# A depthwise convolution that reads its projection from PSUM instead of from a padded copy, in a two-layer hybrid backbone

## The chip, the cores and the metric

The kernel runs on one core of a Trainium2 chip. The metric is the device time of one execution in microseconds (us); the kernel before takes 1846.74 us, the median of 3 runs (1846.3 to 1852.83). Engines are called by the names of the profile: PE (matmuls and transposes), DVE, ACT, POOL, and SP, which issues most DMAs.

## The reference

Two layers over 512 tokens and 256 context tokens of 1024 columns. Each layer normalises and modulates its input and projects it for three groups of heads: neighbourhood attention, a bidirectional state-space scan (SSD), and grouped-query attention (GQA). Then come an output projection and a gated feed-forward block. The change lies in the SSD group, where 1024 projected channels pass a five-tap convolution along the tokens and a silu:

```python
def depthwise_conv(x, w, bias):
    y = lax.conv_general_dilated(x, w[:, None, :], window_strides=(1,),
                                 padding=[(SSD_CONV // 2, SSD_CONV // 2)],
                                 dimension_numbers=('NWC', 'WIO', 'NWC'),
                                 feature_group_count=x.shape[-1])
    return y + bias
...
    def prep(v):
        z, xbc, dt_raw = jnp.split(v, [SSD_WIDTH, SSD_WIDTH + SSD_CONV_CH], axis=-1)
        xbc = jax.nn.silu(depthwise_conv(xbc, conv_w, conv_b))
        xs, bm, cm = jnp.split(xbc, [SSD_WIDTH, SSD_WIDTH + SSD_GROUPS * SSD_STATE], axis=-1)
...
    z, xs, bm, cm, dt = prep(u)
    zc, xsc, bmc, cmc, dtc = prep(u_c)
```

`prep` runs on the tokens and on the context apart, so each of the two sequences has its own zero padding of two columns at either end.

## The kernel before, in words

Channels lie on the 128 partitions and tokens along the free dimension: 512 tokens, then 256 context tokens. The 1024 channels are eight blocks of 128, and `p_xbc(b)` (L749) makes block b in each layer; the text calls the blocks p0 to p7. In the second layer p6 and p7 need only the 512 tokens.

A block runs like this. `wblk` loads 1024 columns of weights and splits them into a high part `wh` (ACT, L326) and a low part `wl` (DVE, L327). `wh` and `wl` have three buffers each, so the split for a block must wait until PE has finished the block three before. `proj_ws` (L338) sums 48 matmuls, 24 of 512 columns and 24 of 256, into a tile `S` of PSUM (24 matmuls where the context is left out). `S` has two buffers. ACT copies the result into a padded tile `MA` in SBUF (L758 and L761), between zeros that DVE writes (L756, L757, L760). DVE makes the first tap with the bias (L763) and adds four more (L768), 770 columns each, into `MB`. ACT takes the tanh (L772) into `MA`, and DVE multiplies (1 + tanh) by the sum (L774 and L776, "the gates"), which with weights halved beforehand is silu. For p0 to p5 six transposes on PE (L785) and two copies on ACT (L791) bring the result into token order.

Other work is woven between the blocks. Three head transposes, tr0 to tr2, turn 128 columns of normalised GQA heads per token block with six or four PE transposes into an `S` tile too (L695); the result is read by ACT (L282) and DVE (L283), and only then is that `S` buffer free. Their inputs come from a rope and a norm on POOL and DVE (L683 to L688). `p_z` projects the gate z after and between the last blocks (L352), through small tiles `sm` and `PT`, with an evacuation on ACT (L805) and DVE (L806). In the first layer POOL and ACT also make the modulation of the second layer under all this: `mod_dots` multiplies 128x512 tiles on POOL (L228) and sums them on ACT (L229). Rows of POOL's L269 are a power that norms need.

Nobody writes the order by hand: a scheduler places every instruction on its engine by its own estimate of times, and each engine then runs its list strictly in that order. An instruction that must wait holds up all that is behind it on its engine.

Of the kernel before, what the change touches and what calls it, by code (L numbers as in the profile page):

```python
# [28 lines left out]
def hybrid_kernel(ctx: ExitStack, tc: tile.TileContext, a, out, dbg=None):  # L29
# [55 lines left out]
    class Split:  # L85
        """columns 0 .. 511 in one bank of PSUM, the others in another"""
# [11 lines left out]

    WB = {"wr": 2, "wh": 3, "wl": 3}
# [7 lines left out]
    # ---------------------------------------------------------- constants  # L107
# [42 lines left out]
    # ---------------------------------------------------------- modulation  # L150
# [8 lines left out]
    def mod_loads(l, c, tags):  # L159
        """512 columns of the modulation weights in tiles of the given tags, one or two k per tile"""  # L160
# [12 lines left out]
    def mod_chunk(l, c, w):  # L173
        """columns 512 c .. 512 c + 511 of the modulation; four row groups of the array take four k"""
# [21 lines left out]
    def mod_rows():  # L196
        """silu of both conditioning vectors as rows on every partition, in four tiles (vector, half)"""
# [11 lines left out]
    def mod_dots(l, c, rows, ptile, aside):  # L209
        """the same columns as mod_chunk by products along rows of the transposed weights"""  # L210
# [50 lines left out]
    # ---------------------------------------------------------- helpers  # L261
# [29 lines left out]
    def spread(rstd, n):  # L291
        """per-token values as a row on every partition"""
        pb = ps_sm()
        for tb in range(n // P):
            PE.matmul(
                pb[:, tb * P : (tb + 1) * P], lhsT=rstd[:, tb : tb + 1].to_broadcast([P, P]),
                rhs=ident, start=True, stop=True,
            )
        pbs = T(sb, "pr", 3, [P, NX])[:, 0:n]
        S.activation(pbs, pb[:, 0:n], AF.Copy)  # L300
        return pbs

    def make_h(l, xT, h, pbs, part, shi, sc):
        """norm, scale and shift of one part of the tokens"""
# [25 lines left out]
    def proj_ws(pt, wh, wl, xh, xl, nk, segs, ks=None):  # L330
        """pt[:, seg] = W^T x, W stationary (nk blocks of 128 rows)"""
# [13 lines left out]
    def proj_as(pt, ws, n, kper, xh, xl, t):  # L345
        """pt[:, :n] = x[t]^T W, activations stationary"""
# [28 lines left out]
    def attn(V2, xk, kts, qcols, bias, yout):  # L375
        """two heads and two blocks of queries; xk: range of x keys (or None); kts: key tiles for P V.
        Returns the steps of the four units: scores and softmax, transposes, and P V where one is complete"""
# [70 lines left out]
    # ---------------------------------------------------------- initial load and transpose  # L448
# [44 lines left out]
    for l in range(L):  # L493
# [9 lines left out]
        # ------------------------------------------------------ norm 1  # L503
# [6 lines left out]
        # ------------------------------------------------------ NA projections  # L510
# [77 lines left out]
        # ------------------------------------------------------ NA attention  # L588
# [50 lines left out]
        # ------------------------------------------------------ GQA projections  # L639
# [9 lines left out]
        def head_in(pt, i, t):  # L649
            """keep 128 columns (two heads) of token block t and their sums of squares"""  # L650
# [69 lines left out]
        # ------------------------------------------------------ GQA attention  # L720
# [24 lines left out]
        # ------------------------------------------------------ SSD: projections, conv  # L745
# [3 lines left out]
        def p_xbc(b):  # L749
            conly = last and b >= 6  # L750
            w = wblk(6 + b)
            pt = ps_s()
            proj_ws(pt, w[0], w[1], hh, hl, KB, xsegs if conly else asegs)
            cp = ma()
            wid = 512 if conly else 770
            V.memset(cp[:, 0:2], 0.0)  # L756
            V.memset(cp[:, 514:516], 0.0)  # L757
            S.activation(cp[:, 2:514], pt[:, 0:512], AF.Copy)  # L758
            if not conly:
                V.memset(cp[:, 772:774], 0.0)  # L760
                S.activation(cp[:, 516:772], pt[:, 512:768], AF.Copy)  # L761
            ac = mb()
            V.tensor_scalar(  # L763
                out=ac[:, 0:wid], in0=cp[:, 0:wid], scalar1=convw[l][:, b, 0:1], scalar2=convb[l][:, b : b + 1],
                op0=ALU.mult, op1=ALU.add,
            )
            for j in range(1, 5):
# [603 lines left out]
```

## Time and profile before

| | us |
|---|---|
| median of 3 runs | 1846.74 |
| lowest, highest | 1846.3, 1852.83 |
| span of the profiled execution | 1843.3 |
| first layer, from the last matmul of p1 to the last of z (164.0 to 301.4) | 137.4 |
| second layer, the same stretch (1211.43 to 1290.8) | 79.37 |

The span runs from the first to the last instruction of one execution; it is 3.4 us under the median of the runs. Over the whole span PE is busy 94%, DVE 60%, ACT 37% and POOL 23%. The two stretches in the table are those in which the eight blocks, the head transposes and z are made. [...]

### The profile page before, as it was taken

To read this page: it belongs to the slowest core of one execution; us is meant where nothing else is said; L and a number is where in the kernel's file an instruction comes from. 1 tells how busy PE (TensorE), PEld (TensorE's weight loads), DVE (VectorE), ACT (ScalarE), POOL (GpSimd) and SP (SyncE) were. 2 spreads that over 40 slices of the span, in tenths; PEclk is the share of its full clock that TensorE was granted. 3 is DMA by queue.
4 is the path that set the end of the run, shared out by engine and by line. 5 is a ranking of instruction groups with operands and counts; after the bars stand their busy time and mean duration, and the time that the engine had idled before them with its cause. 6 is when DMAs were issued, how large, how long until landed. Compare 5 with 4: busy or idle time off the path is not lost.

```text
span 1843.3 us, 26677 instructions
## 1 busy us (share of the span) xinstructions
PE 1737.0 (94%) x10146; PEld 1478.4 (80%) x10146; DVE 1104.0 (60%) x2209; ACT 681.5 (37%) x1386; POOL 423.1 (23%) x429
## 2 busy tenths in 40 slices
PE   7987778989999999999999999999899999999998
PEld 3887667777878888888888887989677788888887
DVE  4559996877475555455654576587786743333334
ACT  5554555556344221121112224334555442232222
POOL 0488886654010000000000002241653100000000
PEclk9998889989989999999999999999999999999999
DMA  9542526433123334333443454342631323333332
GB/s 368 201 139 103 163 89 186 140 90 106 56 75 115 114 115 126 103 116 107 124 129 102 130 163 139 96 131 79 183 105 53 108 90 93 99 96 92 103 100 83
DMA packets 94319, 221.66 MB, mean 120 GB/s; under 512 B 18416, under 2 KB 26224, under 8 KB 94192
## 3 DMA queue, kind: packets, MB, share of 16 engines
q1 hardware_dynamic: 78096, 204.65, 35.6%
q10 hardware_dynamic: 16096, 15.31, 2.5%
q8 instruction: 80, 1.31, 0.3%
q14 instruction: 47, 0.39, 0.1%
HBM read 198.49 MB, written 21.43 MB: 119 GB/s over the span
## 4 chain that ended last, share of the span: by engine, by line
PE 76%; DVE 11%; DMA 5%; ACT 3%; issue 2%; POOL 2%; SPq 0%; ACTq 0%; DVEq 0%; POOLq 0%
PE S L338 61%; PE sm L436 3%; DVE MB L768 2%; DMA wl<-crow 2%; PE PT L424 2%; DVE wl L327 1%; PE PT L338 1%; PE PT L352 1%; PE sm L352 1%; DMA wr<-in_mod_wT_dram 1%; DVE wh L892 1%; PE S L390 1%; ACT wh L326 1%; PE sm L913 1%; PE sm L914 1%
## 5 line engine op out<-in xcount | busy, mean ns | idle before, releaser
L326 ACT ACTIVATE wh<-wr 128x1024 fp32r<-128x1024 f32 (+3 forms) x214 | 207.6, 972 | 732.2 <-PE S L338 542.4
L327 DVE TENSOR_TENSOR wl<-wr,wh 128x1024 fp32r<-128x1024 f32 (+3 forms) x214 | 250.0, 1169 | 174.0 <-ACT wh L326 171.6
L269 POOL TENSOR_TENSOR tiny<-tiny,mhalf 128x2 f32<-128x2 f32 (+2 forms) x17 | 28.7, 1688 | 1067.5 <-DVE tiny L1160 1020.3
L338 PE MATMUL S<-HY,wh 128*128 128x512 f32 (+1 forms) x716 | 214.0, 357 | 5.9 <-ACT HY L318 4.1
L338 PE MATMUL S<-HY,wl 128*128 128x512 f32 (+1 forms) x716 | 214.5, 357 | 0.0
L338 PE MATMUL S<-HZ,wh 128*128 128x512 f32 (+1 forms) x716 | 212.8, 355 | 0.8 <-DVE HZ L319 0.8
L338 PE MATMUL S<-HS,wl 128*128 128x512 f32 (+1 forms) x716 | 213.1, 355 | 0.0
L338 PE MATMUL S<-HS,wh 128*128 128x512 f32 (+1 forms) x716 | 211.1, 353 | 0.0
L231 DVE CUSTOM_DVE_ANT_0 PT<-wr,XFB 128x512 f32<-128x512 f32 x112 | 75.5, 715 | 179.8 <-DMA wr<-in_mod_wT_dram 179.8
L338 PEld LDWEIGHTS S<-HY,wh 128*128 128x128 f32 x716 | 119.8, 192 | 27.2 <-ACT HY L318 4.4
L338 PEld LDWEIGHTS S<-HZ,wh 128*128 128x128 f32 x716 | 118.2, 191 | 21.7 <-DVE HZ L319 2.2
L338 PEld LDWEIGHTS S<-HS,wh 128*128 128x128 f32 x716 | 118.8, 191 | 20.2
L338 PEld LDWEIGHTS S<-HY,wl 128*128 128x128 f32 x716 | 118.8, 191 | 18.8
L338 PEld LDWEIGHTS S<-HS,wl 128*128 128x128 f32 x716 | 118.0, 190 | 18.6
L338 PE MATMUL S<-PHA,wh 128*128 128x512 f32 (+1 forms) x358 | 106.4, 355 | 0.0
L338 PE MATMUL S<-PHB,wh 128*128 128x512 f32 (+1 forms) x358 | 105.0, 351 | 0.0
L338 PE MATMUL S<-GX,wh 128*128 128x512 f32 (+1 forms) x400 | 97.2, 349 | 0.4 <-DVE KA L1114 0.4
L415 POOL TENSOR_SCALAR pr<-pr,tiny 128x640 f32<-128x640 f32 (+2 forms) x80 | 69.3, 869 | 84.0 <-DVE tiny L414 64.3
L768 DVE SCALAR_TENSOR_TENSOR MB<-MA,c,MB 128x770 f32<-128x770 f32 (+1 forms) x64 | 85.3, 1333 | 1.4
L228 POOL TENSOR_TENSOR KA<-QN,XFB 128x512 f32<-128x512 f32 x48 | 73.9, 1546 | 44.3 <-ACT XFB L205 23.5
L424 PE MATMUL PT<-c,pr 128*128 128x128 f32 x384 | 66.5, 289 | 13.4 <-POOL pr L415 4.6
L1261 DVE TENSOR_TENSOR MB<-S,MA 128x768 f32<-128x768 f32 (+1 forms) x42 | 34.6, 823 | 72.6 <-PE S L338 72.5
(402 smaller groups left out, 3911.7 us busy)
## 6 DMA issues: line engine op xcount, KB each, us to landing
wr<-in_mod_wT_dram SPq DMA_DIRECT2D x56, 512.0 KB, 3.7
wr<-in_w_gate_dram SPq DMA_DIRECT2D x44, 512.0 KB, 3.5
wr<-in_w_up_dram SPq DMA_DIRECT2D x44, 512.0 KB, 3.5
wr<-in_w_blk_dram SPq DMA_DIRECT2D x28, 512.0 KB, 3.6
wr<-in_w_down_dram SPq DMA_DIRECT2D x32, 448.0 KB, 3.3
QN<-in_mod_wT_dram SPq DMA_DIRECT2D x48, 256.0 KB, 3.3
wr<-in_w_out_dram SPq DMA_DIRECT2D x32, 256.0 KB, 2.6
wr<-in_w_down_dram SPq DMA_DIRECT2D x16, 512.0 KB, 3.4
```

What stands on the lines that cost most here:

```text
L228: G.tensor_tensor(out=p_, in0=wv, in1=x, op=ALU.mult)
L231: V.tensor_tensor_reduce(out=p_, in0=wv, in1=x, scale=1.0, scalar=0.0, op0=ALU.mult, op1=ALU.add, accum_out=acc[:, o : o + 1],)
L269: POW.tensor_tensor(out=y, in0=v, in1=mhalf[:, 0:n], op=ALU.pow)
L326: S.activation(hi, raw, AF.Copy)
L327: V.tensor_tensor(lo, raw, hi.bitcast(F32), ALU.subtract)
L338: ins = PE.matmul(pt[:, c0:c1], lhsT=w, rhs=xx[:, c0:c1], start=(k == (0 if len(order) == 1 else order[0]) and i == 0), stop=(k == (nk - 1 ...
L352: PE.matmul(pt[:, 0:n], lhsT=s, rhs=w[:, o : o + n], start=(k == 0 and i == 0), stop=(k == KB - 1 and i == 2),)
L415: G.tensor_scalar(out=p_, in0=p_, scalar1=m[:, 4:5], scalar2=1.0, op0=ALU.mult, op1=ALU.mult)
L424: PE.transpose(pt[:, k * P : (k + 1) * P], pr[j, qi][:, kk * P : (kk + 1) * P], ident)
L436: PE.matmul(pv[64 * j : 64 * j + 64, 0:P], lhsT=V2(kts[k], j), rhs=ph[j, qi][:, k, :], start=(k == 0), stop=(k == nkt - 1), tile_position= ...
L768: V.scalar_tensor_tensor(ac[:, 0:wid], cp[:, j : j + wid], convw[l][:, b, j : j + 1], ac[:, 0:wid], ALU.mult, ALU.add)
L1261: V.tensor_tensor(gg[:, c0:c1], pu[:, c0:c1], sg[:, c0:c1], ALU.mult)
```

## The change

The padded copy goes. A small class `Gap` places the context's columns four further right in the `S` tile: tokens in columns 0 to 511, a gap of four in 512 to 515, context in 516 to 771. One memset on DVE zeroes the gap, after the projection. The centre tap with the bias becomes one ACT operation from PSUM into `MB` (Identity with a scale and a bias). The other four taps stay on DVE and read the projection from PSUM, shifted by one or two columns and narrowed at the ends. The tanh is written back into the `S` tile, over the projection, and the gates read it there. `S` has two buffers as before. The second layer's p6 and p7 have no gap and no memset.

```diff
+    class Gap:
+        def __init__(self, t):
+            self.t = t
+        def __getitem__(self, idx):
+            c0, c1 = idx[1].start, idx[1].stop
+            o = 0 if c0 < 512 else 4
+            return self.t[:, c0 + o : c1 + o]
...
-            pt = ps_s()
+            pt = Gap(ps_s())
             proj_ws(pt, w[0], w[1], hh, hl, KB, xsegs if conly else asegs)
-            cp = ma()
-            wid = 512 if conly else 770
-            V.memset(cp[:, 0:2], 0.0)
-            V.memset(cp[:, 514:516], 0.0)
-            S.activation(cp[:, 2:514], pt[:, 0:512], AF.Copy)
+            pt = pt.t
+            wid = 512 if conly else 772
             if not conly:
-                V.memset(cp[:, 772:774], 0.0)
-                S.activation(cp[:, 516:772], pt[:, 512:768], AF.Copy)
+                V.memset(pt[:, 512:516], 0.0)
             ac = mb()
-            V.tensor_scalar(
-                out=ac[:, 0:wid], in0=cp[:, 0:wid], scalar1=convw[l][:, b, 0:1], scalar2=convb[l][:, b : b + 1],
-                op0=ALU.mult, op1=ALU.add,
+            S.activation(
+                ac[:, 0:wid], pt[:, 0:wid], AF.Identity, scale=convw[l][:, b, 2:3], bias=convb[l][:, b : b + 1]
             )
-            for j in range(1, 5):
+            for j in (0, 1, 3, 4):
+                s0, s1 = max(0, 2 - j), wid - max(0, j - 2)
                 V.scalar_tensor_tensor(
-                    ac[:, 0:wid], cp[:, j : j + wid], convw[l][:, b, j : j + 1], ac[:, 0:wid], ALU.mult, ALU.add
+                    ac[:, s0:s1], pt[:, s0 + j - 2 : s1 + j - 2], convw[l][:, b, j : j + 1], ac[:, s0:s1],
+                    ALU.mult, ALU.add,
                 )
-            th = cp
+            th = pt
             S.activation(th[:, 0:wid], ac[:, 0:wid], AF.Tanh)
             o = ac if b < 4 else slot("GT" if b < 6 else "GC")
             V.scalar_tensor_tensor(o[:, 0:512], th[:, 0:512], 1.0, ac[:, 0:512], ALU.add, ALU.mult)
             if not conly:
-                V.scalar_tensor_tensor(o[:, 512:768], th[:, 514:770], 1.0, ac[:, 514:770], ALU.add, ALU.mult)
+                V.scalar_tensor_tensor(o[:, 512:768], th[:, 516:772], 1.0, ac[:, 516:772], ALU.add, ALU.mult)
```

Line numbers move with it: in the changed kernel the memset is L768, the centre tap L770, the other taps L775, the tanh L780, the gates L782 and L784, the transposes of a block L793; `wh` is L337, `wl` L338, a projection L349, a head transpose L706 and its readers L293 and L294. A buffer of `S` is now held from a block's first matmul to its gates, no longer only to the copy. The scheduler makes a new order from all this. In the assigned buffers, a head transpose now takes the `S` buffer of a block whose gates come just before it, and the next block but one takes the same buffer behind the head transpose.

PE in the second layer, at the end of p1. Before (`S_11130` is p1, `S_11224` is tr0, `S_11245` is p2):

```order
L338 MATMUL S_11130<-HS_10206,wl_11127 128x256
L843 MATMUL sm_11728<-dA_11698,c_214 128x96 x3
L695 MATMUL S_11224<-c_66,GR_10653 128x128 x6
L843 MATMUL sm_11728<-dA_11698,c_214 128x96
L843 MATMUL sm_11728<-dA_11698,ones 128x96
L338 MATMUL S_11245<-HY_10199,wh_11241 128x512
```

The same place now (`S_11085` is p1, `MB_11037` the finished p0, `S_11174` tr0, `S_11195` p2):

```order
L349 MATMUL S_11085<-HS_10166,wl_11082 128x256
L851 MATMUL sm_11650<-dA_11620,c_214 128x96 x4
L851 MATMUL sm_11650<-dA_11620,ones 128x96
L793 MATMUL PT_11046<-c_66,MB_11037 128x128 x3
L793 MATMUL PT_11051<-c_66,MB_11037 128x128 x3
L706 MATMUL S_11174<-c_66,GR_10613 128x128 x6
L349 MATMUL S_11195<-HY_10159,wh_11191 128x512
```

The six transposes of p0 have moved from the middle of p2 to the place ahead of tr0 and p2.

DVE in the second layer, from the gates of p1 on. Before (`MA_11179` is the padded copy of p1, `MA_11300`'s source `MA_11294` that of p2, `S_11339` tr1):

```order
L327 TENSOR_TENSOR wl_11530<-wr_11527,wh_11529 128x1024
L763 TENSOR_SCALAR MB_11300<-MA_11294,c_214 128x770
L774 SCALAR_TENSOR_TENSOR MB_11185<-MA_11179,MB_11185 128x512
L776 SCALAR_TENSOR_TENSOR MB_11185<-MA_11179,MB_11185 128x256
L768 SCALAR_TENSOR_TENSOR MB_11300<-MA_11294,c_214,MB_11300 128x770
L283 TENSOR_TENSOR pr_11345<-S_11339,pr_11344 128x512
```

Now (`S_11085` is p1, `S_11195` p2, `S_11284` tr1, whose buffer p3 takes next):

```order
L782 SCALAR_TENSOR_TENSOR MB_11135<-S_11085,MB_11135 128x512
L784 SCALAR_TENSOR_TENSOR MB_11135<-S_11085,MB_11135 128x256
L695 TENSOR_TENSOR pr_11268<-pr_11268,pr_11269 128x512
L697 TENSOR_TENSOR GR_10615<-pr_11268,tiny_1912_10979 128x512
L768 MEMSET S_11195 128x4
L338 TENSOR_TENSOR wl_11465<-wr_11462,wh_11464 128x1024
L775 SCALAR_TENSOR_TENSOR MB_11245<-S_11195,c_214,MB_11245 128x770
L294 TENSOR_TENSOR pr_11290<-S_11284,pr_11289 128x512
L775 SCALAR_TENSOR_TENSOR MB_11245<-S_11195,c_214,MB_11245 128x771 x2
```

The gates of p1 have moved ahead of everything that waits for the end of p2, and the read of tr1 now stands behind the memset of p2, a split of weights and p2's first tap.

ACT in the first layer, at the second block. Before (`MA_1899` is the padded copy of p1, its last row the tanh):

```order
L282 ACTIVATE pr_1954<-S_1947 128x768
L229 ACTIVATE QN_967,tiny_924<-QN_967 128x512
L535 DMA gq_1958<-pr_1954 128x768
L229 ACTIVATE QN_974,tiny_924<-QN_974 128x512
L535 DMA gq_1960<-pr_1955 128x768
L229 ACTIVATE KA_1056,tiny_1053<-KA_1056 128x512
L772 ACTIVATE MA_1899<-MB_1905 128x770
```

Now (`S_1845` is p1, `S_1937` tr0):

```order
L293 ACTIVATE pr_1944<-S_1937 128x768
L240 ACTIVATE QN_960,tiny_924<-QN_960 128x512
L546 DMA gq_1948<-pr_1944 128x768
L240 ACTIVATE KA_976,tiny_924<-KA_976 128x512
L240 ACTIVATE QN_967,tiny_924<-QN_967 128x512
L546 DMA gq_1950<-pr_1945 128x768
L240 ACTIVATE KA_1056,tiny_1053<-KA_1056 128x512
L780 ACTIVATE S_1845<-MB_1895 128x772
```

The tanh of p1 keeps its place behind a run of modulation sums (L229 before, L240 now), each of which waits for a product of POOL's; there is one more between the read of tr0 and the tanh.

## Rows read from the trace of the kernel before

**Rows 1.** Windows: stretch and length, each engine's busy time, PEclk, DMA share, GB/s.
```profile
164.00:301.40 137.40, 105.49 (x642) 95.08 (x643) 117.21 (x136) 68.35 (x175) 107.05 (x73) 0.86 0.42 133
1211.43:1290.80 79.37, 76.71 (x507) 69.54 (x506) 64.88 (x112) 32.40 (x61) 20.29 (x19) 1.00 0.35 106
```
**Rows 2.** Waits of PE, 164 to 301.4: releaser, total us, times, longest.
```profile
PE PT L785 <- DVE MB L774: 14.0, 3, 9.3
PE PT L785 <- DVE GT L774: 6.9, 2, 4.5
PE S L695 <- DVE GR L686: 4.5, 1, 4.5
PE PT L352 <- ACT SA L852: 4.3, 1, 4.3
```
**Rows 3.** Waits of PE, 1194 to 1291.
```profile
PE PT L785 <- DVE MB L774: 1.4, 1, 1.4
PE S L338 <- ACT MA L761: 1.1, 1, 1.1
```
**Rows 4.** Groups of DVE by form, 164 to 284: busy us, mean ns, idle before.
```profile
L768 DVE SCALAR_TENSOR_TENSOR MB<-MA,c,MB 128x770 f32<-128x770 f32 x28 | 47.0, 1680 | 0.6
L763 DVE TENSOR_SCALAR MB<-MA,c 128x770 f32<-128x770 f32 x7 | 8.9, 1270 | 0.0
```
**Rows 5.** Timeline of DVE, 268 to 280: start, us, engine, line.
```profile
277.92 0.41 DVE L806 SCALAR_TENSOR_TENSOR SA<-SA,PT 128x256 f32<-128x256 f32 x1
...
279.63 1.52 DVE L776 SCALAR_TENSOR_TENSOR GC<-MA,MB 128x256 f32<-128x256 f32 x1
```
**Rows 6.** Timeline of DVE, 1237 to 1246 (POOL idle during the taps).
```profile
1238.79 0.68 DVE L283 TENSOR_TENSOR pr<-S,pr 128x512 fp32r<-128x512 f32 x1
1239.39 4.17 DVE L768 SCALAR_TENSOR_TENSOR MB<-MA,c,MB 128x770 f32<-128x770 f32 x4
...
1245.09 0.42 DVE L776 SCALAR_TENSOR_TENSOR MB<-MA,MB 128x256 f32<-128x256 f32 x1
...
1245.79 1.23 DVE L327 TENSOR_TENSOR wl<-wr,wh 128x1024 fp32r<-128x1024 f32 x1
```
**Rows 7.** Groups of ACT by form, 164 to 301.4.
```profile
L229 ACT ACTIVATE QN<-QN 128x512 f32<-128x512 f32 x28 | 17.5, 626 | 9.1 <-POOL QN L228 4.2 <-POOL KA L228 2.4 <-DVE SA L806 2.3
L326 ACT ACTIVATE wh<-wr 128x1024 fp32r<-128x1024 f32 x8 | 8.4, 1046 | 1.0 <-PE S L338 0.8 <-issue 0.2
L772 ACT ACTIVATE MA<-MB 128x770 f32<-128x770 f32 x8 | 6.8, 846 | 34.3 <-DVE MB L768 34.3
L282 ACT ACTIVATE pr<-S 128x768 fp32r<-128x768 f32 x3 | 2.4, 809 | 7.2 <-PE S L695 7.2
```
**Rows 8.** Timelines of PE, first layer, where blocks and their transposes start.
```profile
175.85 0.99 PE L338 MATMUL S<-HY,wh 128*128 128x512 f32 x2
...
208.38 0.62 PE L338 MATMUL S<-HY,wh 128*128 128x512 f32 x2 [0.25 <-ACT MA L761]
...
258.36 0.28 PE L352 MATMUL sm<-wh,HY 128*128 128x256 f32 x1
```
**Rows 9.** Windows with PE's clock (columns as in rows 1).
```profile
168.70:179.00 10.30, 5.35 (x20) 4.09 (x20) 10.27 (x19) 3.42 (x10) 6.67 (x5) 0.50 0.31 102
...
251.00:257.00 6.00, 5.65 (x19) 4.87 (x20) 5.90 (x7) 5.04 (x16) 6.00 (x5) 0.50 0.50 162
```
**Rows 10.** Timeline of PE, second layer, at the start of p2.
```profile
1211.43 0.80 PE L843 MATMUL sm<-dA,c 128*128 128x96 f32 x6
1212.07 0.82 PE L695 MATMUL S<-c,GR 128*128 128x128 f32 x6
...
1213.15 0.62 PE L338 MATMUL S<-HY,wh 128*128 128x512 f32 x2
```
**Rows 11.** Timeline of PE, 1219.5 to 1221, the middle of p2.
```profile
1219.56 0.52 PE L338 MATMUL S<-PHA,wh 128*128 128x512 f32 x2
1219.91 0.51 PE L338 MATMUL S<-HS,wl 128*128 128x512 f32 x2
```

## The prediction

> **What bounds the kernel now.** I read the windows first, because the two layers differ there. In the first layer's convolution stretch PE works 105.5 of 137.4 us, at a mean clock of 0.86, while DVE works 117.2 and POOL 107.1. In the second layer's PE works 76.7 of 79.4 us at full clock [rows 1]. So the first stretch has some 32 us of idle PE and the second under 3: a saving on DVE can only pay in the first, and a new wait of PE costs its full length in the second.
>
> PE's waits say what the 32 us are: the transposes of finished blocks wait for the gates (14.0 + 6.9), tr0 for the norm of its heads (4.5), z once for its evacuation (4.3) [rows 2]. The second layer has two waits, 1.4 and 1.1 us [rows 3].
>
> Then the groups of DVE by form. In the first layer a tap takes 1.68 us and the first tap 1.27 [rows 4]; in the second, with POOL idle, four taps take 4.17 us, 1.04 each [rows 6]. The difference goes with POOL. A gate of 256 columns out of SBUF took 1.52 us in the stretch where POOL is busy, while a product of the same shape with one operand in PSUM took 0.41 [rows 5]; the same gate takes 0.42 where POOL rests [rows 6]. So I take PSUM reads of DVE as untouched by POOL.
>
> **The change, part by part.**
>
> *Taken from ACT and DVE.* Per block two copies, two or three memsets and the first tap on DVE go; one memset and one ACT operation of 772 columns come. The latter I price as the tanh of 770, 0.85 us [rows 7], about what the two copies took together, so ACT is even. No row shows ACT writing PSUM; it reads PSUM at 0.81 for 768 columns and works SBUF to SBUF at 0.85 for 770 [rows 7]. I take 0.85 for the new tanh; the bounds are 0.6 and 1.1 us, a quarter of a microsecond either way per block, under 2 us a layer.
>
> *Cheaper on DVE, first layer.* Seven first taps of 1.27 go: 8.9 us. Twenty-eight taps fall from 1.68 to 1.04: 17.9 us [rows 4, 6]. With one operand in PSUM the gates should not go up to 1.52 any more. So 27 us or more leave DVE's 117 [rows 1], and DVE stops being the fullest engine. The lower end is a tap in PSUM that still meets POOL at `MB`'s side, 1.68, and leaves only the 8.9 us.
>
> The rows on PSUM speak for the change. [...]
>
> *What PE gets back in the first layer.* The chain of a block is now in PSUM: centre tap 0.85, four taps 4.2, tanh 0.85, gates 1.1 (0.69 and 0.42), together 7 us and more with handovers. The order puts the tanh of p1 behind modulation sums, each of which waits for a product on POOL (the ACT group L229 idles 9.1 us for that [rows 7]), so I take 8 to 11 us there. Step by step:
> - The transposes of p0 wait 4.5 us now. Its four taps are done earlier, and the wait goes: p0's transposes start near 164.4 instead of 168.5.
> - tr0 waits 4.5 us for a norm on DVE and POOL [rows 2]. Less work is ahead of it: I take 172.5 instead of about 175.
> - p2 must now wait until tr0 is read out of the buffer that both use: ACT 0.81, DVE 0.68 to 0.95, behind what is queued on both, some 4 to 5 us. It starts at about 177.5 instead of 175.85 [rows 8].
> - The 9.3 us wait of p1's transposes [rows 2] goes, since p1's chain runs from 166 to about 180. In its place p3 waits some 5 us for tr1's readout and starts at 195 to 200, where it starts at 197.2 now; p4 likewise, at 210 to 216 instead of 208.4 [rows 8].
> - p4 to p7 have no head transposes between them. The waits on the GT gates (6.9) and on `SA` (4.3) [rows 2] mostly go, with the half-speed stretches behind them. After such gaps the clock is granted at 0.50: 10.3 us after the first, 6 us after the gap near 250 [rows 9]; of the second, 5.65 us of matmuls at half speed would take 2.8 at full. p7 ends at 251 to 257 instead of 258.4.
> - z then takes the 43 us from 258.4 to 301.4 [rows 1, 8] less its own 4.3 us wait and about 3.3 for the half-speed stretch behind it, 35.5, and ends at 287 to 292.
>
> That is a gain of 9 to 14; I take **12**. The upper bound is that PE gets all four waits back, 30 us [rows 2], the lower bound nothing.
>
> *What PE loses in the second layer.* PE has no slack there, and a buffer of `S` is now held until the gates.
> - p2. After p1 ends at 1211.43 [rows 10], ACT splits weights (1.05 [rows 7]) and DVE makes `wl` (1.23 [rows 6]); the order has this `wl`, and a memset that waits for p1's end, ahead of the gates of p0. The gates end at 1214.7. Six transposes take 0.8, tr0's six 0.8, as in [rows 10], ACT's readout 0.8 behind two copies out of the transposes, DVE's readout 0.95. p2 starts at about 1218.5 instead of 1213.15 [rows 10]: 5.3 later, of which 0.8 are transposes that it no longer makes in its middle. **+4.5.**
> - p3 and p4. tr1 follows p2 at once, but its reader on DVE is queued behind the memset of p2, a `wl` whose `wh` waits for the same end of p2, and p2's first tap: 1.05 + 1.23 + 1.04 + 0.68 [rows 6, 7], with the overlap at their ends about 4.1 us, of which tr1 itself is 0.6. p3 starts 3.5 us late; p4 likewise behind tr2. **+7.0.** Before, the same reads lay beside p3's matmuls, since tr1 and p3 had different buffers.
> - p5 to p7 take a buffer whose gates ended during the block between: a projection lasts 24 pairs of 0.35, 8.4 us [rows 11], and a chain without POOL 7 to 8. Nothing, up to 1 us each if the chain is late.
> - The old wait of 1.1 us on the copy [rows 3] goes: **−1.1.** Sum +10.4.
> - The clock. Gaps of 4.5 and 2.4 us brought it to 0.50 in the first layer [rows 2, 9], gaps of 1.4 and 1.1 did not in the second [rows 1, 3]. Three new gaps of 3.5 to 5 us lie on the side that falls. The cost of one is 2.7 (half of 5.35) and 2.8 by [rows 9], less where the stretch is short; I take 1.7, in all **+5**, between 0 and 8.
>
> *Sum.* −12 + 10.4 + 5 = +3.4 on a span of 1843.3; with the 3.4 us by which the runs' median exceeds the span, **1850.1 us**. Between the layers and in attention the order moves a little too; I leave that at nothing, plus or minus 3.
>
> **The rivals.**
> *The second layer decides (slower).* What the first layer gains is lost again there to ACT: the tanh of every block stands behind POOL's products, the buffer is not free, and each of p2 to p4 waits longer than 5 us, while in the second layer every gap costs a fall of the clock. First layer −2, second +10.4 + 8: +16.4, about 1863. It decides if PE's waits for a buffer in the first layer reach the 25 us that the waits removed are worth. For it: the idle time of ACT for POOL. Against it: ACT is half empty there. [...]
>
> *The first layer decides (faster).* DVE freed of 27 us lets the waits of PE in the first layer go almost wholly, with the falls of the clock behind them: −22 (four waits of 30 us [rows 2], less 8 for three readouts). With the second layer at +8, no falls: −14, about 1833. For it: DVE and POOL are fuller than PE there. Against it: the order has the readouts on the path in both layers.
>
> *Taps in PSUM are slowed by POOL all the same.* Then the first layer's gain is from 8.9 us of first taps only, about −4, and the sum is +11.4, about 1858. The rows of one shape speak against it [rows 5, 6].
>
> **How the numbers follow.** Forecast 0.5, the slower rival 0.2, the faster 0.2, taps slowed 0.1. A measurement of this kernel can tell about 0.5%, 9.2 us, from no change: under 1837.5 is faster, over 1856 slower. The forecast's bounds (gain 6 to 18, loss 8 to 19) put it between 1837 and 1860: 0.04 faster, 0.40 same, 0.06 slower. The slower rival counts slower, the faster one 0.16 faster and 0.04 same, taps slowed 0.06 slower and 0.04 same. Sums: faster 0.20, same 0.48, slower 0.32. The range 1833 to 1865 leaves out the outer parts of both rivals.
>
> **What would show it.** Right: taps in the first layer near 1.04 us; p2 of the second layer about 5 us later than now, two more gaps of about 3.5 us ahead of p3 and p4, with a granted clock of 0.50 behind them; z of the first layer done near 290. Wrong: no gap ahead of p3 in the second layer; the tap still at 1.7 us in the first; PE waiting over 25 us in the first layer for `S` buffers; or a difference of several microseconds outside the two stretches.

## The result, and the profile after

| | us | ratio to before, 95% interval |
|---|---|---|
| before, median of 8 runs | 1846.52 (1841.97 to 1852.83) | |
| changed kernel, median of 8 runs | 1858.57 (1847.27 to 1866.29) | 1.0062 (1.0041 to 1.0083) |
| the same, second series of 8 runs, beside 1844.15 for before | 1854.0 (1844.72 to 1860.23) | 1.0054 (1.0032 to 1.0075) |

The change makes the kernel slower by about 0.6%, some 11 us: on the side that the forecast of 1850 named, 8.6 us beyond it, and inside the range. By the prediction's own bound of 0.5% it counts as slower, to which it had given a chance of 0.32, and not as "same", its likeliest case. The profiled execution of the changed kernel took 1851.41 us with a span of 1849.6, so it is one of the quicker ones. I therefore compare stretches, and several profiles of each.

First the page of the changed kernel, its span and part 1:

```profile
span 1849.6 us, 26616 instructions
...
PE 1735.0 (94%) x10146; PEld 1478.7 (80%) x10146; DVE 1060.7 (57%) x2161; ACT 683.7 (37%) x1372; POOL 396.1 (21%) x429
```

DVE lost 43 us of work and POOL 27, and the kernel did not get faster. The windows of the two convolution stretches (the stretch and its length, busy time of the engines, PEclk, which is the clock granted to PE as a share of its full speed, DMA share, GB/s) say where the two went:

```profile
164.00:298.20 134.20, 103.45 (x665) 93.68 (x664) 87.22 (x122) 71.50 (x171) 92.79 (x78) 0.89 0.46 142
1199.46:1290.55 91.09, 81.15 (x506) 73.14 (x505) 54.53 (x93) 33.18 (x55) 13.62 (x20) 0.94 0.30 92
```

Beside [rows 1] the first layer's DVE work fell from 117 to 87 us, and the second layer's stretch grew from 79.4 to 91.1, its clock falling from 1.00 to 0.94. The two windows of the first layer do not begin at the same place in the work: the last matmul of p1 starts at 162.7 us before and at 165.3 now. From there to the end of z it is 138.9 us before and 132.6 now, 6.3 us less. The waits of PE in the first layer's stretch (releaser, total us, times, longest), which answer to [rows 2]:

```profile
PE S L349 <- DVE pr L294: 19.3, 3, 12.2
PE S L706 <- DVE GR L697: 7.1, 1, 7.1
PE PT L793 <- DVE GT L782: 2.3, 1, 2.3
PE PT L793 <- DVE MB L782: 1.7, 2, 1.3
```

The waits on gates fell from 21 us to 4. In their place p2, p3 and p4 wait 19.3 us until a head transpose has been read out of the buffer that they take. In the second layer, which answers to [rows 3]:

```profile
PE S L349 <- DVE pr L294: 8.3, 3, 3.1
PE PT L793 <- DVE MB L782: 1.7, 1, 1.7
```

The timeline of DVE there, at the end of p2, shows the queue that the prediction named: memset, weight split, first tap, and only then the readout L294 for which p3 waits.

```profile
1215.33 0.06 DVE L768 MEMSET S<- 128x4 f32 x1 [3.21 <-PE S L349]
1216.03 1.23 DVE L338 TENSOR_TENSOR wl<-wr,wh 128x1024 fp32r<-128x1024 f32 x1 [0.63 <-ACT wh L337]
1217.17 1.01 DVE L775 SCALAR_TENSOR_TENSOR MB<-S,c,MB 128x770 f32<-128x770 f32 x1
1218.10 0.68 DVE L294 TENSOR_TENSOR pr<-S,pr 128x512 fp32r<-128x512 f32 x1
```

On PE the same place reads (tr1, then p3):

```profile
1215.09 0.60 PE L706 MATMUL S<-c,GR 128*128 128x128 f32 x4
1218.84 0.82 PE L349 MATMUL S<-HY,wh 128*128 128x512 f32 x2 [3.15 <-DVE pr L294]
```

Last, the groups of DVE by form in the first layer (164 to 284), which answer to [rows 4]:

```profile
L338 DVE TENSOR_TENSOR wl<-wr,wh 128x1024 fp32r<-128x1024 f32 x8 | 22.2, 2772 | 8.6 <-ACT wh L337 8.6
L775 DVE SCALAR_TENSOR_TENSOR MB<-S,c,MB 128x771 f32<-128x771 f32 x15 | 15.2, 1016 | 0.2
L775 DVE SCALAR_TENSOR_TENSOR MB<-S,c,MB 128x770 f32<-128x770 f32 x15 | 15.2, 1011 | 0.2
```

A tap fell from 1.68 us to 1.01. But a weight split, two operands out of SBUF, now takes 2.77 us on average, where it took 1.81 before. One of the eight took 8.16 and one 4.00; the other six average 1.7.

### The profile page after: what moved, and what is told of

Its sections match the earlier page's. It is cut to its first block, busy times and chain, and to the rows that moved or that the text cites. A ratio compares the mean times of both kernels' runs of the same rounds, so it can differ in the third digit from the quotient of the medians.

```text
span 1849.6 us, 26616 instructions
## 1 busy us (share of the span) xinstructions
PE 1735.0 (94%) x10146; PEld 1478.7 (80%) x10146; DVE 1060.7 (57%) x2161; ACT 683.7 (37%) x1372; POOL 396.1 (21%) x429
## 4 chain that ended last, share of the span: by engine, by line
PE 75%; DVE 10%; DMA 7%; ACT 3%; issue 3%; POOL 1%; SPq 0%; ACTq 0%; DVEq 0%; POOLq 0%
PE S L349 56%; DMA wr<-in_mod_wT_dram 3%; PE sm L447 3%; PE PT L363 3%; DMA wl<-crow 2%; PE sm L363 2%; DVE wl L338 2%; PE PT L435 2%; PE S L401 1%; PE PT L349 1%; PE sm L921 1%; PE sm L922 1%; DVE PT L242 1%; PE PT L966 1%; ACT wh L337 1%
## 5 line engine op out<-in xcount | busy, mean ns | idle before, releaser
L337 ACT ACTIVATE wh<-wr 128x1024 fp32r<-128x1024 f32 (+3 forms) x214 | 207.7, 972 | 716.1 <-PE S L349 511.4
L338 DVE TENSOR_TENSOR wl<-wr,wh 128x1024 fp32r<-128x1024 f32 (+3 forms) x214 | 259.6, 1214 | 189.1 <-ACT wh L337 187.2
L349 PE MATMUL S<-HY,wh 128*128 128x512 f32 (+1 forms) x716 | 217.2, 362 | 32.0 <-DVE pr L294 27.6
L349 PE MATMUL S<-HZ,wh 128*128 128x512 f32 (+1 forms) x716 | 214.9, 359 | 1.1 <-DVE HZ L330 1.1
L349 PE MATMUL S<-HY,wl 128*128 128x512 f32 (+1 forms) x716 | 214.6, 358 | 0.0
L349 PE MATMUL S<-HS,wh 128*128 128x512 f32 (+1 forms) x716 | 209.6, 350 | 0.0
L349 PE MATMUL S<-HS,wl 128*128 128x512 f32 (+1 forms) x716 | 209.3, 350 | 0.0
L349 PEld LDWEIGHTS S<-HY,wh 128*128 128x128 f32 x716 | 121.4, 196 | 53.9 <-DVE pr L294 29.2
L349 PEld LDWEIGHTS S<-HZ,wh 128*128 128x128 f32 x716 | 120.1, 194 | 21.1 <-DVE HZ L330 1.7
L349 PEld LDWEIGHTS S<-HY,wl 128*128 128x128 f32 x716 | 120.2, 194 | 19.3
L349 PEld LDWEIGHTS S<-HS,wh 128*128 128x128 f32 x716 | 116.8, 188 | 19.0
L349 PEld LDWEIGHTS S<-HS,wl 128*128 128x128 f32 x716 | 116.6, 188 | 18.5
L349 PE MATMUL S<-PHA,wh 128*128 128x512 f32 (+1 forms) x358 | 105.1, 351 | 0.0
L349 PE MATMUL S<-PHB,wh 128*128 128x512 f32 (+1 forms) x358 | 104.5, 350 | 0.0
L349 PE MATMUL S<-GX,wh 128*128 128x512 f32 (+1 forms) x400 | 97.1, 348 | 0.4 <-DVE KA L1122 0.4
L349 PEld LDWEIGHTS S<-GX,wh 128*128 128x128 f32 x400 | 65.6, 188 | 11.2 <-DVE KA L1122 0.8
L239 POOL TENSOR_TENSOR KA<-QN,XFB 128x512 f32<-128x512 f32 x48 | 64.1, 1339 | 41.7 <-ACT XFB L216 22.9
```

Of the source, the lines that this page charges most:

```text
L239: G.tensor_tensor(out=p_, in0=wv, in1=x, op=ALU.mult)
L337: S.activation(hi, raw, AF.Copy)
L338: V.tensor_tensor(lo, raw, hi.bitcast(F32), ALU.subtract)
L349: ins = PE.matmul(pt[:, c0:c1], lhsT=w, rhs=xx[:, c0:c1], start=(k == (0 if len(order) == 1 else order[0]) and i == 0), stop=(k == (nk - 1 ...
```

## The experiments

All were timed against the kernel before, in three series in which its median was 1844.15 to 1846.19 us. Every profile was cut at the same places: the first matmul of p0, the last of z, and the last state product of the scan (`PT<-XFB,GB`) that is woven into the attention behind it; that last stretch is called the attention here. The lengths in us, each from one profiled execution:

| kernel | first layer p0 to z | second layer p0 to z | second layer's attention | ratio, 95% interval |
|---|---|---|---|---|
| before | 155.9 | 96.5 | 98.1 | |
| changed | 149.5 | 108.2 | 104.6 | 1.0062 (1.0041 to 1.0083) |
| second_look | 149.6 | 108.4 | 102.6 | 1.0054 (1.0032 to 1.0075) |
| new_first | 143.6 | 95.3 | 94.3 | 0.9944 (0.9922 to 0.9965) |
| new_second | 154.1 | 107.8 | 105.0 | 1.0117 (1.0098 to 1.0137) |
| own_bank | 149.8 | 98.4 | 102.9 | 0.9988 (0.9973 to 1.0002) |
| own_bank_b45 | 144.0 | 97.0 | 101.4 | 0.9947 (0.9916 to 0.9978) |
| tanh_sbuf | 143.4 | 108.0 | 94.0 | 0.9978 (0.9962 to 0.9994) |
| noprod_old | 113.5 | 95.3 | 96.1 | 0.9792 (0.9745 to 0.9839) |
| noprod_new | 126.6 | 95.2 | 95.5 | 0.9867 (0.9821 to 0.9913) |
| first_own | 135.1 | 96.3 | 95.0 | 0.9846 (0.9832 to 0.9861) |
| first_own_tanh | 126.9 | 96.0 | 93.6 | 0.9872 (0.9853 to 0.9891) |
| own_all | 139.8 | 96.3 | 104.3 | 0.9943 (0.9922 to 0.9964) |
| own_all_tanh | 132.0 | 93.7 | 96.7 | 0.9859 (0.9841 to 0.9877) |

The expectations measure a stretch from the end of p1, 17 us later than this table does. What lies around the stretches moves too: the first matmul of p0 comes at 145 to 155 us, and the first layer's attention takes 123 to 132. The two noprod kernels leave work out and had two runs each.

### second_look: the changed kernel once more

> The changed kernel once more, unedited, for a second profile of it. Theory A (the result is made in the two convolution stretches, and their waits belong to the order): the first layer's stretch, from the last matmul of p1 to the last of z, again takes about 133 us, the second layer's about 91 us, ratio near 1.006. Theory B (the longest wait of the first layer, 12.2 us ahead of p4, comes from one weight split on DVE that took 8.16 us while POOL ran its products back to back, and depends on how the two engines happen to meet): that split takes another time here, anything from 1.2 to 8 us, and the first layer's stretch moves by as much, to between 126 and 134 us. The 4.4 us that the first layer's feed-forward block took less than before, and the 6.2 us that the second layer's attention took more, recur if they belong to the order, and do not if they belong to one execution.

Both stretches came out as before, 149.6 and 108.4 us. The attention of the second layer was again long, so that belongs to the change. The gain around the first layer's feed-forward block did not recur: from the last state product of the first layer to p0 of the second it was 764 us, against 759 in the first profile and 765 before. It belongs to that one execution. The 8.16 us split came again, at the same place and of the same length, which speaks against theory B. The timeline of DVE in this run:

```profile
216.08 8.17 DVE L338 TENSOR_TENSOR wl<-wr,wh 128x1024 fp32r<-128x1024 f32 x1 [2.11 <-ACT wh L337]
224.18 1.00 DVE L775 SCALAR_TENSOR_TENSOR MB<-S,c,MB 128x770 f32<-128x770 f32 x1
225.11 0.94 DVE L294 TENSOR_TENSOR pr<-S,pr 128x768 fp32r<-128x768 f32 x1
```

But own_bank, below, speaks for it. Its first layer has the same order as the changed kernel's on PE, DVE, ACT and POOL, and there the split at this place took 1.80 us and the next one 8.37:

```profile
209.71 1.80 DVE L338 TENSOR_TENSOR wl<-wr,wh 128x1024 fp32r<-128x1024 f32 x1 [1.99 <-ACT wh L337]
225.54 8.37 DVE L338 TENSOR_TENSOR wl<-wr,wh 128x1024 fp32r<-128x1024 f32 x1 [0.64 <-ACT wh L337]
```

So the order alone does not fix where the long split falls.

### new_first and new_second: one layer each

```diff
+            if not last:
+                pt = Gap(ps_s())
...
+            else:
+                pt = ps_s()
+                proj_ws(pt, w[0], w[1], hh, hl, KB, xsegs if conly else asegs)
+                cp = ma()
```

new_first has the new convolution in the first layer and the old one in the second; new_second has `if last` instead.

> The new convolution in the first layer, the padded copy of before in the second. Theory A (gain of 6 us in the first layer's stretch, loss of 11.7 in the second's): faster than before by 4 to 12 us, ratio 0.994 to 0.998; the second layer's stretch back at 79 to 80 us and no wait of a projection for the readout of a head transpose there. Rival (the first layer's gain is one lucky execution and is worth nothing on the median): ratio 0.999 to 1.002.

> The padded copy of before in the first layer, the new convolution in the second. Theory A: slower by what the second layer's stretch loses, 11.7 us, and by up to 6 more if the attention behind it loses too: ratio 1.006 to 1.010. Rival (the loss comes from the first layer, where the changed order meets POOL): ratio 0.999 to 1.002, the second layer's stretch still longer by some 11 us but made up elsewhere.

Theory A held on both signs. The first layer alone gains 0.56%, 10.3 us of the 1844.15 that before took beside it; the second alone costs 1.17%, 21.6 us, a little more than theory A allowed. The sum, +11.3, is about what the whole change costs. The second layer's price is 11.3 us in the stretch and 6.9 in the attention of that profile; the remaining 3.4 lie around them.

### own_bank: tr1 and tr2 of the second layer in a tile of their own

```diff
         def head_tr(i, n):
-            pt = ps_s()
+            pt = ps_t() if n <= 512 else ps_s()
```

> The changed kernel, with the two head transposes of 512 columns (tr1 and tr2 of the second layer) put into a PT tile of one bank, so that p3 and p4 no longer wait for their readout. The first layer's order is untouched. Theory A (p3 and p4 lose 3.2 us each to the readout of a head transpose that shares their buffer): both waits go, the second layer's stretch takes 91 less 6.4, so 84 to 86 us, and with it the fall of the clock behind them; ratio to before 1.001 to 1.005, 4 to 9 us faster than the changed kernel. Rival (the buffer itself, held from the first matmul to the gates, is what p3 and p4 wait for): a wait of 2 to 4 us for the gates of p1 and p2 takes the place of the old one, the stretch stays at 90 us or more, ratio 1.005 to 1.008.

The waits of PE in its second layer's stretch:

```profile
PE S L349 <- DVE pr L294: 2.0, 1, 2.0
PE PT L793 <- DVE MB L782: 1.7, 1, 1.7
```

Two of the three readout waits are gone, no wait for a gate came in their place, and the stretch is 98.4 us, 9.8 less than in the changed kernel: more than the 6.3 us of the waits, because the clock stayed up. Its stretch from the end of p1 is granted 0.98:

```profile
1203.50:1285.00 81.50, 77.84 (x507) 70.99 (x506) 56.12 (x93) 33.38 (x56) 14.12 (x20) 0.98 0.33 104
```

So the convolution in PSUM costs little in the second layer, 1.9 us more than before; sharing a buffer with the head transposes costs 10 us. Stretch and ratio came out slightly better than theory A said (81.5 us against 84 to 86, 0.9988 against 1.001 or more).

### own_bank_b45 and the attention

As own_bank, with the old convolution for p4 and p5 of the second layer:

```diff
+            if not last or b < 4 or b >= 6:
+                pt = Gap(ps_s())
...
+            else:
+                pt = ps_s()
```

> As own_bank, with the padded copy of before for p4 and p5 of the second layer. The scheduler's order in the second layer's attention is then close to that of before. Theory A (5 to 8 us of the loss lie in the attention, where the order that follows from the change puts a state product behind the transposes whose tile it takes, and is no matter of the convolution itself): the attention after the last z takes 94 to 100 us, where own_bank took 102.9 and before 98.1; ratio to before 0.991 to 0.997. Rival (the attention is longer because the clock, or the transfers, come out of the convolution in another state): it stays at 102 to 105 us, ratio 0.998 to 1.001.

The attention took 101.4 us, between the two bands: undecided by itself, although the ratio is where theory A put it. The other runs tell more. In eleven profiles the order of PE in this attention is, but for buffer numbers, exactly the changed kernel's or the kernel before's. With the changed kernel's order (changed, second_look, new_second, own_bank, own_all) it took 102.6 to 105.0 us; with the order of before (before, new_first, both noprod, first_own, first_own_tanh) 93.6 to 98.1. But the first five also have the new convolution in the second layer and the other six have not. Two kernels part the causes: tanh_sbuf and own_all_tanh have the new convolution there and an order like neither, and took 94.0 and 96.7. And own_all, whose longest wait in its convolution stretch is 1.6 us, still took 104.3. So the order is the likely cause, and neither the convolution itself nor its waits; no run changed the order alone. What differs first, on PE before:

```profile
1297.28 0.44 PE L390 MATMUL S<-KA,QN 128*128 128x384 f32 x1 [1.95 <-ACT pr L410]
...
1297.97 1.35 PE L958 MATMUL PT<-XFB,GB 128*128 128x256 f32 x4
```

and in the changed kernel:

```profile
1297.31 1.84 PE L966 MATMUL PT<-XFB,GB 128*128 128x256 f32 x4 [2.93 <-ACT PHA L439]
1299.08 0.69 PE L447 MATMUL sm<-PHA,GV 128*64 128x128 f32 x2
1299.70 0.69 PE L401 MATMUL S<-KA,QN 128*128 128x384 f32 x1
```

A state product has moved ahead of a set of scores and waits for the copy that frees its tile. From 1304 to 1332 us the clock was then granted 0.70 in the changed kernel:

```profile
1304.00:1332.00 28.00, 23.73 (x140) 19.68 (x141) 15.91 (x50) 12.01 (x29) 15.26 (x18) 0.70 0.52 148
```

and 0.94 before:

```profile
1304.00:1332.00 28.00, 24.34 (x188) 19.69 (x187) 20.32 (x61) 15.07 (x39) 16.67 (x21) 0.94 0.54 147
```

PE was about as busy and made 140 matmuls in that time, where it had made 188. From 13 to 41 us after the last z the five profiles with this order were granted 0.70 to 0.76, the six with the order of before 0.94 to 1.00. That the first moved row is what starts this is not shown: tanh_sbuf has a wait of 2.6 us at the same row, and its attention took 94.0.

### tanh_sbuf: the buffer comes free after the taps

```diff
-            th = pt
+            th = ma()
```

> The changed kernel, with the tanh written to a tile MA in SBUF and the gates reading it there, so that a buffer of S comes free after the taps, some 2 us earlier; taps and centre tap stay in PSUM. Theory A (with two buffers of S, a head transpose and the next projection share the one that the block in work does not hold, whatever the tanh does): p3 and p4 of the second layer still wait 2 to 3 us each for the readout, the stretch takes 87 to 91 us, ratio to before 1.002 to 1.007. Rival (the tanh in PSUM holds the buffers and makes the loss): the two waits go, the stretch takes 80 to 83 us, ratio 0.994 to 0.999.

In the second layer theory A held: readout waits of 7.4 us, a stretch of 91.0 us from the end of p1. The tanh in PSUM is not what makes that loss. Yet the kernel is by the ratios 14 us faster than the changed one and a little faster than before, for reasons outside it: the first layer gained 6 us (no split in its stretch took over 2.4 us) and the attention, in another order again, 10. The ratio so fell between the two theories; the stretch separates them.

### noprod_old and noprod_new: no products on POOL

```diff
-                        G.tensor_tensor(out=p_, in0=wv, in1=x, op=ALU.mult)
-                        S.activation(p_, p_, AF.Copy, accum_out=acc[:, o : o + 1])
+                        S.activation(p_, wv, AF.Copy, accum_out=acc[:, o : o + 1])
```

Two theories of the first layer's gain stand against each other: that DVE's operations no longer meet POOL's products (a tap of 1.01 us where it was 1.68), and the rival, that the first tap and the memsets have left DVE.

> The kernel before, without POOL's products of the modulation in the first layer: ACT sums the weights as they were loaded, so the second layer's modulation is left out of the computation in effect. Both theories: the taps on DVE fall from 1.68 to about 1.04 us and no weight split takes longer than 1.5 us; the first layer's stretch shrinks from 139 to between 100 and 120 us. It is the base for the next run.

> The same products left out, with the new convolution in the first layer and the padded copy in the second (as in new_first). [...] Rival (it gains because the first tap and the memsets have left DVE): the stretch is 3 to 9 us shorter than in noprod_old.

Without the products the old convolution takes 113.5 us in the first layer and the new one 126.6: the new one is 13 us slower, 3 more than the 10 that I had allowed the first theory, where the rival had it 3 to 9 us shorter. From the end of p1, as the expectation counts, the old one takes 96.4 us, less than the 100 to 120 expected; its taps average 1.06 us and no split takes over 1.5. The waits of PE in noprod_new's first layer look like the changed kernel's in the second (the base has none on the readout):

```profile
PE S L348 <- DVE pr L293: 8.6, 3, 3.2
PE PT L819 <- DVE MB L782: 0.6, 1, 0.6
```

So the change gains in the first layer only while POOL makes the products. They cost the old convolution 42 us (155.9 less 113.5), the new one 17 to 23. Two things limit what the pair shows. ACT's sums, 46 to 48 us of its work in the stretch, now end before p0, so DVE's meeting with POOL is not all that was taken away. And the old convolution is then bound by PE, busy 111.8 of 113.5 us at full clock:

```profile
153.10:266.60 113.50, 111.84 (x752) 101.99 (x751) 79.85 (x141) 40.36 (x79) 25.99 (x25) 1.00 0.36 112
155.10:281.60 126.50, 117.33 (x750) 106.84 (x750) 71.70 (x123) 40.78 (x69) 23.87 (x25) 0.95 0.32 99
```

The first row is noprod_old, the second noprod_new. With so little idle time on PE no saving on DVE could pay, so the rival, that the first tap and the memsets leaving DVE make the gain, is not excluded. How the gain divides between it and the faster taps (by [rows 4] 8.9 and 17.9 us of DVE's work) is not shown.

### first_own, first_own_tanh, own_all and own_all_tanh: head transposes in their own tiles

```diff
         def head_tr(i, n):
-            pt = ps_s()
+            pt = ps_s() if last else Split()
...
-                pr_ = [(0, n)]
+                pr_ = [(0, n)] if last or n <= 512 else [(0, 512), (512, n)]
```

This is first_own, on top of new_first; `Split` (a class, no weight split) puts columns 0 to 511 in `PT` and the rest in `sm`, and the readout takes the two parts one after the other. own_all does it in both layers of the changed kernel. The two with tanh have `th = ma()` besides.

> As new_first (new convolution in the first layer, padded copy in the second), with the first layer's head transposes in tiles PT and sm instead of a buffer of S. Theory A (what keeps the first layer's gain small is the 17.8 us that p2, p3 and p4 wait for the readout of a head transpose in their buffer): these waits go and the first layer's stretch falls from 127 to between 108 and 120 us, ratio to before 0.985 to 0.991. Rival (behind them stand the chains themselves, late on ACT and DVE because of POOL): new waits on gates and on the heads' norm take their place, the stretch stays at 122 to 128 us, ratio 0.992 to 0.996.

> As first_own, with the first layer's tanh in SBUF. Theory A: a buffer comes free 2 us sooner, and the gates meet POOL again (up to 1.5 us for the short one instead of 0.41): the two about cancel, the stretch within 4 us of first_own's. Rival (the tanh in PSUM costs a good part of the gain, since it holds S behind ACT's queue): 5 to 10 us less than first_own.

> The changed kernel in both layers, with all head transposes of both layers in PT and sm. Theory A (the shared buffer is the loss): the second layer's stretch 79 to 83 us and the first's 108 to 120, the attention of the second layer still 95 to 105 as its order falls; ratio to before 0.983 to 0.995. Rival (own tiles collide with the transposes of the blocks, which use PT too): second layer's stretch 85 us or more, ratio 0.995 to 1.003.

> As own_all, with the tanh of both layers in SBUF. Theory A: no projection waits for a buffer any more in the second layer (stretch 77 to 80 us); ratio to before 0.982 to 0.992. Rival (the DVE chain, not the buffer, is late): second layer's stretch 82 us or more, ratio 0.992 to 1.0.

first_own is the fastest kernel that does the whole work: 1817.66 us, 28 us under before. Its first layer's stretch is 135.1 us from p0, 118 by the measure of the expectation. PE's waits there no longer name a buffer of `S`:

```profile
PE PT L820 <- DVE MB L783: 9.1, 3, 5.5
PE PT L820 <- DVE GT L783: 3.2, 1, 3.2
PE sm L878 <- DVE pr L294: 2.7, 1, 2.7
```

Theory A held for first_own, though new waits for gates took part of the old ones' place, as its rival said. For own_all it held in the second layer, whose stretch is back at 96.3 us, 79.2 from the end of p1; the first layer's stretch, 122.7 from there, missed the band of 108 to 120 and lies in first_own's rival's. Against first_own it loses in the second layer's attention (104.3 against 95.0), as its order is the changed kernel's, and 5 us in the first layer's stretch; in its profile p0 also came 6 us later and the first attention took 4 us more. first_own_tanh took 8 us less in the stretch, as its rival said, and gave 8 back in the attention of the first layer (131.4 us against 123.6): no gain. own_all_tanh has the shortest stretch in the second layer, 93.7 us, which is 76.7 by the measure of its expectation, just under theory A's band.

## Why the prediction was right

**Sign and size.** Forecast +3.4 us on the span, from −12 in the first layer and +15.4 in the second. By new_first and new_second the layers measured about −10 and +22. In the changed kernel's own profile the two stretches measured −6.4 and +11.7, and the attention behind the second +6.5, which was not in the sum. The mechanism in both stretches is the one forecast. That the sum stayed inside the range owes something to luck: the second stretch was priced 3.7 us too high, which hid part of the first layer's missing gain and of the attention. By the time alone the rivals at 1858 and 1863 were nearer than the forecast; the traces decide against them.

**Taps in PSUM.** Taken as 1.04 us, measured 1.01 to 1.02 with POOL at work; the gates at 0.69 and 0.41. A tap out of PSUM is no longer than one out of SBUF was without POOL, 1.04 [rows 6]. The third rival, taps that POOL slows all the same, is out, although its 1858 us is what was measured. That faster taps are the whole gain of the first layer is not shown: noprod_old and noprod_new show only that without POOL's products there is none.

**Centre tap and tanh.** Priced at 0.85 us each. The centre tap measured 0.98 and the tanh into PSUM 0.81.

**First layer, step by step.** Relative to p0, which came 2.6 us later: transposes of p0 forecast at 164.4, measured 164.4; tr0 172.5 and 172.4; p2 177.5 and 177.8; p3 195 to 200 and 195.1; p4 210 to 216 and 218.8. At p4 the step failed. The readout of tr2 stood behind the 8.16 us weight split, the wait was 12.2 us instead of 5, and z ended at 295.3 instead of 287 to 292. The profile so shows a gain of 6.4. new_first, whose order there is the same, has the long split and a wait of 11.6 us too, but reached p4 at 215.4 and z's end at 289.3 on this count, inside both bands; it gained 12.3 in its profile and 10.3 by its times. Where the two part is told in the last section.

**Second layer's stretch.** p2 started 6.4 us after the end of p1 where it had been 1.7, so 4.7 later, less 0.8 for the moved transposes: 3.9 against a forecast of 4.5. p3 and p4 waited 3.15 us each, forecast 3.5. Two falls of the clock followed, behind p3 and p4: 3.36 us of work at 0.54 and 5.67 at 0.52 cost by estimate 1.5 and 2.7 us, together 4.3 against 5. No fall followed the waits ahead of p2 (1.7 and 2.0 us): the clock is 1.00 from there to p3. With the 2.5 us of old waits [rows 3] gone, 3.9 + 6.3 + 4.3 − 2.5 = 12.0, and the stretch grew by 11.7. own_bank shows that the cause is the one named. Two single waits of 3.15 us for a PSUM buffer stand ahead of the two falls (PEclk 0.94 for the stretch; 0.98 in own_bank, which has neither).

**The term that failed.** "Between the layers and in attention the order moves a little too; I leave that at nothing, plus or minus 3." In every profile with that order the attention of the second layer took 4.5 to 6.9 us longer than the 98.1 of before. I had compared the order only around the convolution. A difference of several microseconds outside the two stretches was one of the signs of being wrong that the prediction named, and it came.

**The rivals.** "The second layer decides" named the right layer, but its first half did not come: the first layer kept a gain, and PE's waits for a buffer there were 19.3 us, under the 25 that the rival needed. "The first layer decides" was wrong for this kernel; first_own comes close to its picture once the readouts are off the path.

## What to carry to other kernels

Reading a matmul's result in PSUM instead of copying it out does two things: it spares DVE's operations the meeting with POOL (a tap of 1.01 us out of PSUM, 1.68 out of SBUF, both beside POOL's products), and it holds the accumulator until the last reader is done. Price both by stage: with a buffer shared with the head transposes it paid 10 us where POOL was busy, cost 22 where PE was the bound, and cost 13 in the first layer too once POOL's products were gone and PE was the bound there. With few accumulators look for who else takes one: moving the head transposes to other tiles turned +0.6% into −0.6% with the new convolution in both layers, and −0.6% into −1.5% with it in the first alone. Where a scheduler makes the order, compare the order behind the change too, not only around it.

## What the runs showed of the hardware that I had not expected

A DVE operation with two operands in SBUF, a weight split, stood through a whole run of POOL's. The split takes 1.2 us alone [rows 6], and up to 2.3 beside POOL in the stretch of the kernel before. In the changed kernel one of them starts at 211.40 and takes 8.16 us, to 219.56. POOL's timeline:

```profile
210.83 1.29 POOL L239 TENSOR_TENSOR KA<-QN,XFB 128x512 f32<-128x512 f32 x1
...
215.72 1.54 POOL L609 TENSOR_TENSOR GR<-GR,c 128x768 f32<-128x768 f32 x1
217.20 1.28 POOL L239 TENSOR_TENSOR QN<-QN,YO 128x512 f32<-128x512 f32 x1
223.96 2.55 POOL L239 TENSOR_TENSOR KA<-QN,XFB 128x512 f32<-128x512 f32 x2 [5.48 <-DMA QN<-in_mod_wT_dram]
```

POOL runs on at 1.28 to 1.29 us a product, no slower than the product at 207.10, 1.33 us in idle time of DVE, until it waits for a DMA at 218.48; the split ends 1.1 us after that, about its own length. In the stretch of the kernel before both were slowed instead, 1.68 us a tap and on average 1.70 to 1.73 a product. So the two get in each other's way in both kernels; but this split of 8.16 us lasted past the end of six POOL operations in a row, of which five started after it.

Such splits need neither the new convolution nor the tanh in PSUM. Some 25 us ahead of p0 one of 5.0 to 6.5 us stands in all twelve profiles with POOL's products, the kernel before among them, and it too ends 1.1 us after POOL stops. Before, DVE's row and POOL's two around its pause:

```profile
120.40 6.42 DVE L327 TENSOR_TENSOR wl<-wr,wh 128x1024 fp32r<-128x1024 f32 x1 [0.99 <-ACT wh L326]
125.27 0.46 POOL L673 TENSOR_TENSOR pr<-GR,c 128x128 f32<-128x128 f32 x1
127.54 1.00 POOL L667 TENSOR_TENSOR GR<-GR,c 128x128 f32<-128x128 f32 x1 [1.81 <-ACT GR L651]
```

The prediction could have read it there. In the first layer's stretch splits of 7.6 to 8.4 us came in all seven profiles with the new first layer, the tanh in PSUM and POOL's products (own_all has one of 6.9 besides), and in none of the others, where the longest was 2.4; without POOL's products the longest was 1.5. Why POOL's run holds up a split to its end in the one case and only slows it in the other stays open: no run set the moment at which it starts.

The same meeting parts the profiles with one order. With the changed kernel's order of the first layer its stretch took 143.6 and 144.0 us in new_first and own_bank_b45, and 149.5 to 149.8 in the changed kernel, second_look and own_bank. The eight small products of a rope on DVE, out of SBUF, take 0.2 us each in the first two, where POOL waits for a DMA just then; in the other three, three or four of them take 1.3 us each, as long as a product of POOL's. The changed kernel, then new_first:

```profile
182.67 4.54 DVE L694 TENSOR_TENSOR pr<-GR,c 128x64 f32<-128x64 f32 x8 [1.39 <-DMA gq<-pr]
180.84 1.17 DVE L694 TENSOR_TENSOR pr<-GR,c 128x64 f32<-128x64 f32 x8 [1.82 <-DMA gq<-pr]
```

Behind them on DVE stand the gates of p1, and only in the three longer profiles do the transposes in p2 wait for gates, 1.3 to 3.1 us. That is where the profiles part; the rest of the 6 us was not traced.
